# One core, q·kᵀ for 96 heads: the last head's store split between the GpSimd queue and the SP queue

## The chip, the cores and the metric

The kernel runs on one core of one Trainium2 chip. The metric is device time in microseconds (us), lower is better. One profiled execution of the kernel gives the trace; the plain executions give the time.

## The reference

The kernel computes, for every batch and head, the raw attention scores: `out[b,h,i,j] = sum over d of q[b,h,i,d] * k[b,h,j,d]`, in float32, with 8 batches, 12 heads, a sequence of 1024 and a head dimension of 64.

```python
def reference(q, k):
    return np.einsum('bhid,bhjd->bhij', q, k).astype(np.float32)
```

The inputs are 2 x 25 MB, the output is 96 heads x 1024 x 1024 x 4 bytes, some 403 MB. There is no softmax and no scaling: nearly all bytes that the kernel moves are the output's.

## The kernel before

**Heads and blocks.** Batch and head are one axis of 96 heads (`of` is the output as 96 x 1024 x 1024). They are handled in blocks of 2, 2, 4, 8, 8 and then six times 12 heads. For each block q and k are loaded (`load`, L66, or `load_head`, L78, for the first two blocks), cast to 16-bit by GpSimd (`cast_rows`, L90; `cast_quads`, L113), transposed (by TensorE for the first two blocks, by VectorE for all others, L145) and then used head by head. The loads of a later block are issued in the midst of an earlier one (`LOADS`, L263), by ScalarE's queue.

**One head.** `scores` (L156) makes the 1024 x 1024 scores of one head in an SBUF tile `o_sb` of 128 partitions x 8 rows x 1024 columns. Partition p holds rows 8p to 8p+7 of the head (the index t in the code), so each partition's 32 KB are contiguous in DRAM. From the second head on the head goes in four steps u = 0 to 3 of two rows t each: eight matmuls fill a PSUM tile of 128 x 2048 (L171), and one ScalarE copy takes it to `o_sb` (L181). After the fourth copy one DMA of 4 MB, issued by SP, stores the head (L184 to L189):

```python
out=of[self.first + n].rearrange("(p t) j -> p (t j)", p=P),
in_=o_sb.rearrange("p t j -> p (t j)"),
```

This is 128 rows of 32 KB, one for each partition, and the trace has them as 128 packets of 32 KB on the 16 DMA engines, eight to an engine.

**What orders the work.** Every instruction is pinned to program order (`pin`), so each engine runs its list as written; the framework only adds the waits. `out_pool` has three buffers, so the first copy of a head waits until the store of the head three before it has landed. SP issues nothing but the stores after the first loads, each behind the wait for its head's last copy. GpSimd's list ends with the casts of the last block. When all lists are at their end, SP waits at the end of the program (L304) for the landing of every DMA, and a barrier of the five engines closes it.

Of the kernel before, what the change touches and what calls it, by code (L numbers as in the profile page):

```python
# [10 lines left out]
P = 128  # L11

@with_exitstack
def kernel(
# [6 lines left out]
    nc = tc.nc  # L21
# [3 lines left out]
    BH = B * H  # L25
# [5 lines left out]
    of = out.rearrange("b h i j -> (b h) i j")  # L31
# [3 lines left out]
    PE_BLOCKS = 2  # L35
    NMAX = max(sizes)
    CHUNK = 48 * 32

    consts = ctx.enter_context(tc.tile_pool(name="consts", bufs=1))
    ident = consts.tile([P, P], F16)  # L40
# [6 lines left out]
    pin = tc.keep_in_program_order  # L47

    def half_tile():
        half_sb = half_pool.tile([P, CHUNK], F16, tag="half")  # L50
        return half_sb

    class Block:
# [3 lines left out]
        def __init__(self, first, N, by_pe):  # L57
# [5 lines left out]
            self.halves = {}  # L63
            self.cut = max(1, self.R * 32 // CHUNK + (self.R * 32 % CHUNK > 0))

# [90 lines left out]
        def scores(self, n, side, ps_pool, w):  # L156

            half, g = divmod(n, self.N // 2)
            cs = slice(half * D, (half + 1) * D)

            qT = self.qT.rearrange("c (g m t) -> c g t m", t=NT, m=P)
            kT = self.kT.rearrange("c (g j) -> c g j", j=S)
            o_sb = out_pool.tile([P, NT, S], F32, tag="out")
            for u in range(NT // w):
                ps = ps_pool.tile([P, w * S], F32, tag="po")
                for tt in range(w):
                    for j in range(2):
                        js = slice(j * 512, (j + 1) * 512)
                        at = tt * S + j * 512
                        pin(  # L170
                            nc.tensor.matmul(  # L171
                                ps[:, at : at + 512],
                                qT[cs, g, w * u + tt],
                                kT[cs, g, js],
                            )
                        )
                dst = o_sb[:, w * u : w * u + w].rearrange("p t j -> p (t j)")
                if w == 1 and u % 2:
                    pin(nc.vector.tensor_copy(out=dst, in_=ps))  # L179
                else:  # L180
                    pin(nc.scalar.copy(out=dst, in_=ps))  # L181
                for do in side.get(u, []):
                    do()
            pin(  # L184
                nc.sync.dma_start(
                    out=of[self.first + n].rearrange("(p t) j -> p (t j)", p=P),
                    in_=o_sb.rearrange("p t j -> p (t j)"),
                )
            )  # L189

    blocks, first = [], 0
    for i, N in enumerate(sizes):
# [116 lines left out]
```

## Time and profile before

| what | value |
|---|---|
| time, median of 3 runs | 1063.17 us (1063.16 to 1063.77) |
| span of the profiled execution, first to last instruction | 1061.2 us |
| median less span | 1.9 us |
| bytes moved, mean rate over the span | 453 MB, 427 GB/s |
| stores | 96 of 4 MB, all by SP; median 21.8 us from issue to landing |
| ScalarE copies to `o_sb` | 384, 1.86 us each for 128 x 2048 |
| TensorE, ScalarE, VectorE, GpSimd busy | 66%, 66%, 44%, 35% |

The profiled execution's own time is its span of 1061.2 us and what lies around it; the plain runs' median is 1.9 us above the span.

The page's slices each cover a fortieth of the span, 26.5 us. The views that the prediction uses are the chain of waits that ends last, the table of stretches (for any stretch of time: what each engine was busy, the share of the 16 DMA engines' time that packets took, and GB/s; a packet is booked where it starts), and the records of single packets and landings on which that table rests. A store's landing is made of 16 records, one for each DMA engine that has finished its part.

### The profile page before, as it was taken

The page shows a single profiled execution, that of the slowest core. Times are in us where ns is not written, and L with a number is a line of the kernel's source. Part 1 is how long each engine was busy: PE and PEld are TensorE (multiplying, and loading weights), DVE is VectorE, ACT ScalarE, POOL GpSimd, SP SyncE. Part 2 cuts the span into 40 slices and gives each one's busy share as a digit, 9 for nine tenths or more (in the row PEclk, how much of TensorE's full clock was granted, in tenths as well). Part 3 has the DMA queues.
Part 4 walks back from the last instruction along what each step waited for, and adds up shares of the span by engine and source line. Part 5 has one row for each costly group of instructions (what it writes and reads, how often), then busy time and mean ns, then how long its engine had stood idle before and what let it go on. Part 6 is the DMA issues. An engine that isn't in the chain of part 4 may idle for free.

```text
span 1061.2 us, 4282 instructions
## 1 busy us (share of the span) xinstructions
PE 701.0 (66%) x1568; PEld 241.5 (23%) x1568; DVE 471.3 (44%) x75; ACT 697.3 (66%) x386; POOL 368.3 (35%) x286
## 2 busy tenths in 40 slices
PE   6866755765677557775577855777557777778770
PEld 2322211221222112221122211222112222222220
DVE  2999502990795007960079600795007950000000
ACT  4866755755677556775577755777557777777771
POOL 6967228607720463304633046320463200000000
DMA  9999999999999999999999999999999999999997
GB/s 375 434 435 434 434 432 429 432 430 429 429 434 431 429 438 429 435 422 428 434 434 433 425 424 437 432 431 426 432 430 434 434 434 430 430 435 430 433 431 319
DMA packets 17588, 453.25 MB, mean 427 GB/s; under 512 B 1952, under 2 KB 1952, under 8 KB 2976
## 3 DMA queue, kind: packets, MB, share of 16 engines
q1 hardware_dynamic: 14688, 406.85, 89.2%
q10 hardware_dynamic: 2880, 46.14, 10.3%
q8 instruction: 12, 0.20, 0.1%
q14 instruction: 8, 0.07, 0.0%
HBM read 50.33 MB, written 402.65 MB: 427 GB/s over the span
## 4 chain that ended last, share of the span: by engine, by line
DMA 71%; ACT 18%; PE 8%; issue 1%; DVE 0%; POOL 0%; ACTq 0%; SPq 0%
DMA out_dram<-o_sb 71%; ACT o_sb L181 18%; PE ps L171 8%; DMA early<-in_q_dram 0%; PE ps L151 0%; POOL half_sb L97 0%; ACTq L181 0%; DVE kT L154 0%; DVE o_sb L179 0%; ACT kT L154 0%; SPq L84 0%
## 5 line engine op out<-in xcount | busy, mean ns | idle before, releaser
L181 ACT COPY o_sb<-ps 128x2048 f32<-128x2048 f32 (+1 forms) x384 | 695.0, 1860 | 334.6 <-DMA out_dram<-o_sb 306.2
L171 PE MATMUL ps<-kT,qT 64*128 64x512 f16 x1536 | 696.9, 617 | 329.2 <-ACT o_sb L181 325.5
L127 POOL CAST half_sb<-x_sb 32x1536 f16<-32x1536 f32 (+1 forms) x256 | 346.5, 1353 | 454.5 <-DMA x_sb<-in_q_dram 315.0
L171 PEld LDWEIGHTS <-qT 64*128 64x128 f16 x1536 | 238.3, 157 | 786.0 <-issue 781.3
L145 DVE STREAM_TRANSPOSE qT<-half_sb 128x1536 f16<-128x1536 f16 (+1 forms) x34 | 232.7, 7140 | 372.0 <-issue 314.9
L145 DVE STREAM_TRANSPOSE kT<-half_sb 128x1536 f16<-128x1536 f16 (+1 forms) x34 | 234.3, 7198 | 0.0
L127 POOL CAST half_sb<-early 32x1024 f16<-32x1024 f32 x16 | 16.5, 1034 | 3.9 <-DMA early<-in_q_dram 3.2
L151 PE MATMUL ps<-ident,half_sb 128*128 128x128 f16 x32 | 4.1, 308 | 6.6 <-POOL half_sb L97 6.0
L154 DVE COPY qT<-ps 128x1024 f16<-128x1024 f16 x2 | 2.5, 1225 | 12.1 <-PE ps L151 12.1
L179 DVE COPY o_sb<-ps 128x1024 f32<-128x1024 f32 x4 | 4.9, 1224 | 4.3 <-PE ps L171 4.3
L97 POOL CAST half_sb<-early 128x512 f16<-128x512 f32 x8 | 4.6, 613 | 4.1 <-DMA early<-in_q_dram 4.1
L151 PEld LDWEIGHTS <-half_sb 128*128 128x128 f16 x32 | 3.2, 139 | 8.4 <-POOL half_sb L97 6.3
L154 ACT ACT_TABLE_LOAD x1 | 1.3, 1283 | 5.6 <-DMA early<-in_q_dram 5.6
L154 DVE COPY kT<-ps 128x1024 f16<-128x1024 f16 x1 | 1.2, 1225 | 4.3 <-PE ps L151 4.3
L154 ACT COPY kT<-ps 128x1024 f16<-128x1024 f16 x1 | 1.0, 1012 | 1.2 <-PE ps L151 1.2
masks.py:199 POOL TENSOR_SCALAR_AFFINE_SELECT ident<-ident 128x128 f16<-128x128 f16 x1 | 0.3, 292 | 0.1
masks.py:197 POOL MEMSET ident<- 128x128 f16 x1 | 0.2, 204 | 0.3 <-POOLq L293 0.3
L293 POOL MEMSET const-float32-0.0<- 128x1 f32 x1 | 0.1, 98 | 0.2 <-issue 0.2
L293 POOL MEMSET const-bfloat16-1.0<- 128x1 bf16 x1 | 0.1, 100 | 0.0
L293 POOL MEMSET const-uint8-127<- 128x1 uint8 x1 | 0.1, 100 | 0.0
L293 POOL MEMSET const-float32-1.0<- 128x1 f32 x1 | 0.1, 98 | 0.0
## 6 DMA issues: line engine op xcount, KB each, us to landing
out_dram<-o_sb SPq DMA_DIRECT2D x96, 4096.0 KB, 21.8
x_sb<-in_q_dram ACTq DMA_DIRECT2D x6, 3072.0 KB, 22.2
x_sb<-in_k_dram ACTq DMA_DIRECT2D x6, 3072.0 KB, 21.9
x_sb<-in_k_dram ACTq DMA_DIRECT2D x2, 2048.0 KB, 19.0
x_sb<-in_q_dram SPq DMA_DIRECT2D x1, 2048.0 KB, 18.2
x_sb<-in_q_dram ACTq DMA_DIRECT2D x1, 2048.0 KB, 18.5
early<-in_k_dram ACTq DMA_DIRECT2D x4, 256.0 KB, 5.0
early<-in_q_dram SPq DMA_DIRECT2D x4, 256.0 KB, 4.7
```

The source lines that it names most:

```text
L97: nc.gpsimd.tensor_copy(out=self.rows[x][:, :, half], in_=self.raw[x][:, half * n : (half + 1) * n].rearrange("p (r d) -> p r d", d=D),)
L127: nc.gpsimd.tensor_copy(out=half_sb[q0 : q0 + 32].rearrange("p (r d) -> p r d", d=32), in_=raw[32 * b : 32 * b + 32, c * m : (c + 1) * m, h],)
L145: pin(nc.vector.transpose(out=dst, in_=src))
L151: pin(nc.tensor.transpose(t_ps[:, t], self.rows[x][:, t], ident))
L154: pin(copy(out=dst, in_=src))
L171: nc.tensor.matmul(ps[:, at : at + 512], qT[cs, g, w * u + tt], kT[cs, g, js],)
L179: pin(nc.vector.tensor_copy(out=dst, in_=ps))
L181: pin(nc.scalar.copy(out=dst, in_=ps))
L293: nc = _bacc.Bacc("TRN2", target_bir_lowering=False, num_devices=1)
```

## The change

For all heads but the last nothing changes: the store is moved into a method of its own, `store`, with the same DMA. For the last head the eight rows t of a partition are seen as `(g h t)` with g, h and t of two each: h = 0 are the rows 0, 1, 4, 5 (made by the copies u = 0 and u = 2), h = 1 are the rows 2, 3, 6, 7 (u = 1 and u = 3).

- The rows h = 0 are stored by two DMAs that GpSimd issues: first for the partitions 126 and 127 (4 pieces of 8 KB), then for the partitions 0 to 125 (252 pieces of 8 KB).
- The rows h = 1 of all 128 partitions are stored by one DMA that SP issues (256 pieces of 8 KB).

The two GpSimd DMAs wait for the third copy of the last head, SP's DMA for the fourth, as the store before did. GpSimd's list gets two instructions longer, SP's keeps its length; no other engine's list changes. At the end SP also waits for the landing of the two GpSimd DMAs.

```diff
+    TAIL = ((126, 128), (0, 126))
...
-            pin(
-                nc.sync.dma_start(
-                    out=of[self.first + n].rearrange("(p t) j -> p (t j)", p=P),
-                    in_=o_sb.rearrange("p t j -> p (t j)"),
-                )
-            )
+            self.store(n, o_sb)
+
+        def store(self, n, o_sb):
+            if self.first + n < BH - 1:
+                pin(
+                    nc.sync.dma_start(
+                        out=of[self.first + n].rearrange("(p t) j -> p (t j)", p=P),
+                        in_=o_sb.rearrange("p t j -> p (t j)"),
+                    )
+                )
+                return
+            dst = of[self.first + n].rearrange(
+                "(p g h t) j -> p g h (t j)", g=2, h=2, t=2
+            )
+            src = o_sb.rearrange("p (g h t) j -> p g h (t j)", g=2, h=2)
+            for a, b in TAIL:
+                pin(nc.gpsimd.dma_start(out=dst[a:b, :, 0], in_=src[a:b, :, 0]))
+            pin(nc.sync.dma_start(out=dst[:, :, 1], in_=src[:, :, 1]))
```

## The prediction

> **What bounds the kernel now.** I read the page from the top, then the chain that ended last, then the last 40 us in stretches.
>
> ```profile
> GB/s 375 434 435 434 434 432 429 432 430 429 429 434 431 429 438 429 435 422 428 434 434 433 425 424 437 432 431 426 432 430 434 434 434 430 430 435 430 433 431 319
> q1 hardware_dynamic: 14688, 406.85, 89.2%
> DMA 71%; ACT 18%; PE 8%; issue 1%; DVE 0%; POOL 0%; ACTq 0%; SPq 0%
> L181 ACT COPY o_sb<-ps 128x2048 f32<-128x2048 f32 (+1 forms) x384 | 695.0, 1860 | 334.6 <-DMA out_dram<-o_sb 306.2
> ```
>
> The stores bound it. The DMA engines move 422 to 438 GB/s in every slice between the first and the last, ScalarE's copies wait for a free output buffer, and the chain is 71% store. Only two slices fall short: the first and the last, 319 GB/s. At 430 GB/s the last slice's bytes would have taken 319/430 x 26.5 = 19.7 us, so 6.8 us are lost there, and the change touches only this slice.
>
> SP's waits, and the timeline of the last matmuls and copies, say the same:
>
> ```profile
> SPq L304 <- DMA out_dram<-o_sb: 21.0, 1, 21.0
> ```
>
> ```profile
> 1034.96 1.86 PE L171 MATMUL ps<-kT,qT 64*128 64x512 f16 x4
> 1035.09 3.64 ACT L181 COPY o_sb<-ps 128x2048 f32<-128x2048 f32 x2 [0.18 <-PE ps L171]
> 1038.75 0.33 SPq L185 DMA_DIRECT2D out_dram<-o_sb  x1
> ```
>
> All computing is done at 1038.73. The last store is issued at 1038.75, and SP then waits 21.0 us for landings. A 4 MB store takes 9.7 us at 430 GB/s, so more than one store's worth was still queued in front of it. So the last store does not wait for its issue; it waits for its turn. The stretches (columns: stretch, its length, busy time of PE, PEld, DVE, ACT, POOL, clock, DMA share, GB/s) show how the queue empties:
>
> ```profile
> 1051.00:1052.00 1.00, 0.00 (x0) 0.00 (x0) 0.00 (x0) 0.00 (x0) 0.00 (x0) 1.00 0.91 393
> 1052.00:1053.00 1.00, 0.00 (x0) 0.00 (x0) 0.00 (x0) 0.00 (x0) 0.00 (x0) 1.00 0.91 393
> 1053.00:1054.00 1.00, 0.00 (x0) 0.00 (x0) 0.00 (x0) 0.00 (x0) 0.00 (x0) 1.00 0.61 262
> 1054.00:1055.00 1.00, 0.00 (x0) 0.00 (x0) 0.00 (x0) 0.00 (x0) 0.00 (x0) 1.00 0.38 164
> 1055.00:1056.00 1.00, 0.00 (x0) 0.00 (x0) 0.00 (x0) 0.00 (x0) 0.00 (x0) 1.00 0.15 66
> 1056.00:1057.00 1.00, 0.00 (x0) 0.00 (x0) 0.00 (x0) 0.00 (x0) 0.00 (x0) 1.00 0.08 33
> 1057.00:1058.00 1.00, 0.00 (x0) 0.00 (x0) 0.00 (x0) 0.00 (x0) 0.00 (x0) 1.00 0.08 33
> 1058.00:1059.00 1.00, 0.00 (x0) 0.00 (x0) 0.00 (x0) 0.00 (x0) 0.00 (x0) 1.00 0.08 33
> 1059.00:1060.00 1.00, 0.00 (x0) 0.00 (x0) 0.00 (x0) 0.00 (x0) 0.00 (x0) 1.00 0.00 0
> ```
>
> 33 GB/s over 1 us is one 32 KB packet. So from 1056 on one packet starts in each microsecond, and by the packet records (1213 ns for 32 KB) all three belong to one DMA engine: it starts its last packets at 1056.16, 1057.37 and 1058.58 and is done at 1059.80. The engine before it is done at 1057.02, the next two at 1056.67 and 1055.87, eight have finished by 1053.8, and the mean of all 16 is 1054.7. The late engine is not a hiccup of the last store: in the landing records it comes 6.7 to 6.9 us after the first engine in each of the last eight stores. It has the same bytes, and enters the last store late. This engine alone sets the end.
>
> After its last packet come the landing at 1060.26 and the closing barrier, to 1061.24: 1.44 us that the change leaves in place. The plain median, 1063.17, is 1.93 us above this span; I make the sum on the span and add 1.93.
>
> **The change, part by part.**
>
> *What the split removes.* SP's last DMA halves: eight packets of 32 KB on each engine become 16 of 8 KB. The early loads show 8 KB packets at 309 ns. Four of them are 1236 ns against 1213 (consecutive packets overlap by some 3.5 ns in either size, so 1222 against 1209.5), that is 12.5 ns more for each 32 KB. A whole store in such pieces costs each engine 8 x 12.5 ns = 0.1 us more. The SP issue itself, 0.33 us at 1038.75, is hidden: the late engine is busy with earlier stores until about 1050.1, the others until 1043.4 or later.
>
> *What the earlier issue brings.* GpSimd's DMAs wait for the third copy (done at 1036.86) instead of the fourth (1038.73): 1.9 us earlier. Worth nothing: DMA share is 0.9 or more up to 1053, so no engine lacks work at that time. GpSimd's list is empty from before 900 us on; nothing stands behind its two DMAs but the closing barrier. Issuing costs GpSimd an unknown time. The nearest rows are SP's issue (0.33 us) and the 256 KB loads on an idle chip, 4.7 to 5.0 us from issue to landing. I take 3 us from the row's 4.7, all hidden: until an engine runs dry without the GpSimd half there are 1053.1 - 4.9 - 1036.9 = 11.3 us, and until it moves the end some 17 us. Were that cover gone, each us beyond it would be a us of time.
>
> *What the two DMAs cost an engine.* Here is the gain or the loss. Total bytes and the engines' speed stay; what can move the end is how the GpSimd half is dealt to the 16 engines. Evenly it is eight partitions each, 16 pieces, 16 x 305.5 ns = 4.89 us. 126 partitions do not go evenly into 16, and no row of this trace shows a GpSimd DMA, so I bound the late engine's share. At best it gets none of the 126: it is 4.89 us earlier, done at 1054.9, and the end passes to the next engine. At worst GpSimd uses few engines: 126 = 14 x 9 = 9 x 14 = 7 x 18, and with 18 partitions an engine carries 36 pieces, 11.0 us instead of 4.89.
>
> The value I take: 14 engines with nine partitions each and the other two partitions on two engines apart, since this is the most even equal split of 126 and nearest to the observed eight to an engine. Then 14 engines have one partition more (2 x 0.31 = 0.62 us later) and two have seven fewer (14 x 305.5 ns = 4.28 us earlier). If the late engine is one of the two, it ends at 1059.80 - 4.28 + 0.1 = 1055.6, and the engine now second sets the end: 1057.02 + 0.62 + 0.1 = 1057.74. That is 2.06 us earlier. At the end SP has one more semaphore to look at, 0.08 us by the gaps between its last waits. Sum: -2.06 + 0.08 = -1.98; the span becomes 1059.26, the time 1061.2 us.
>
> [...]
>
> [...]
>
> **The rivals.**
>
> *A. The late engine keeps its share or nearly so.* For: two of 16 engines are relieved, 14 are not, and nothing in the trace tells which the late one is. Against: the split is uneven, so some engine gains. With nine partitions on it: +0.62 + 0.1 + 0.08 = +0.8, 1064.0 us; with six, -4 x 305.5 ns + 0.18 = -1.0, 1062.1 us.
>
> *B. Slower: GpSimd deals the 126 over few engines.* With nine engines of 14 partitions each carries 12 pieces more, 3.7 us; with seven, 20 pieces more, 6.1 us. If the late engine is among them the end moves by 3.8 to 6.3 us (1067.0 to 1069.5); if not, the one at 1057.02 may be: +1.0 to +3.5 us. It decides from the point at which the late engine carries eight pieces (four partitions) more than now, 12 or more in all. For: 126 is an odd size. Against: the equal split over 14 exists.
>
> *C. GpSimd's half comes late, or the program pays for it elsewhere.* If its first packet reaches the engines after some 1054, the end goes with it; a GpSimd path with a cost of 2 to 5 us outside the covered stretch (at the start, or in the closing barrier) would give 1063 to 1066. Against: the 11 us of cover. For: no row prices it.
>
> *D. Nothing of it shows,* because the halves are dealt as the store was: +0.1 + 0.08, 1063.4 us.
>
> **How the numbers follow.** 0.2% of 1063.17, 2.1 us, is about what a measurement of this kernel can tell from no change; below 1061.0 is faster, above 1065.3 slower. Forecast (late engine relieved by far): 0.44, 1060.2 to 1061.8, the low end if the second engine is relieved too (end at 1056.67 + 0.72, -0.35 more) and the pieces cost nothing, plus some change of the lags between executions. Its centre lies just short of 2.1 us, so I count 0.33 as faster (perfect levelling would end at 1054.7, 5.1 us earlier, which bounds any gain) and 0.11 as within. A and D: 0.32, within. B: 0.14, slower. C: 0.10, of it 0.07 slower. Together: faster 0.33, within 0.11 + 0.32 + 0.03 = 0.46, slower 0.14 + 0.07 = 0.21. The range 1060.2 to 1066.0 leaves out perhaps 0.03 below and 0.16 above. The forecast's own range is 1060.2 to 1061.8.
>
> **What would show it.** Right: in the stretches after, the run of single packets at the end is shorter and starts earlier, the last packet ends near 1057.7, SP's last wait is some 19 us, and on GpSimd's queue two engines have two packets of 8 KB each and 14 have 18. Wrong: a tail of 8 KB packets, four to a 1.2 us, past 1059.8 (A), a GpSimd queue that uses few engines (B), GpSimd packets that begin only after 1048 (C), or a longer closing barrier (C). It would also be wrong if the engine that is late in the profiled execution were not the late one in the plain ones.

## The result and the profile after

The changed kernel is slower: 1065.78 us in the median of 18 runs (1064.39 to 1069.24), against 1063.22 us before (1063.01 to 1063.77). The ratio is 1.0025, with a 95% interval of 1.0018 to 1.0031. That is +2.6 us where -2.0 us was forecast. The runs also scatter over 4.9 us, where those of before scatter over 0.8. The profiled execution of after is one of its faster ones (1064.82 us, span 1062.8), so its +1.6 us of span is less than the median's loss.

What answers to the page's lines of before:

```profile
GB/s 375 434 433 433 433 433 434 434 424 433 437 431 426 430 430 432 434 427 427 434 434 432 421 431 433 432 433 425 429 432 432 433 434 432 431 434 430 431 433 292
q1 hardware_dynamic: 14816, 404.76, 88.6%
q0 software_dynamic: 352, 2.10, 0.5%
DMA 71%; ACT 18%; PE 8%; issue 1%; DVE 0%; POOL 0%; ACTq 0%; SPq 0%
```

Between the first slice and the last the rate is 421 to 437 GB/s, as before (422 to 438), and the last slice falls from 319 to 292 GB/s. q0 is GpSimd's queue: 2.10 MB, the half h = 0, in 352 packets, of which 256 are data (8 KB) and 96 carry 4 bytes.

The issues stand in the timeline, and SP's last wait in its waits:

```profile
1034.98 3.63 ACT L182 COPY o_sb<-ps 128x2048 f32<-128x2048 f32 x2 [0.18 <-PE ps L172]
1037.16 1.45 POOL L201 DMA_DIRECT2D out_dram<-o_sb  x2 [205.76 <-ACT o_sb L182]
1038.64 0.64 SPq L202 DMA_DIRECT2D out_dram<-o_sb  x1
```

```profile
SPq L317 <- DMA out_dram<-o_sb: 21.9, 1, 21.9
```

GpSimd issues its two DMAs in 1.45 us, SP its half in 0.64 us; neither is late. SP waits 21.9 us at the end instead of 21.0. The stretches show what happens in that wait (length, busy times of the engines, clock, DMA share, GB/s). Before:

```profile
1045.00:1053.00 8.00, 0.00 (x0) 0.00 (x0) 0.00 (x0) 0.00 (x0) 0.00 (x0) 1.00 0.98 422
1053.00:1057.00 4.00, 0.00 (x0) 0.00 (x0) 0.00 (x0) 0.00 (x0) 0.00 (x0) 1.00 0.31 131
1057.00:1061.00 4.00, 0.00 (x0) 0.00 (x0) 0.00 (x0) 0.00 (x0) 0.00 (x0) 1.00 0.04 16
```

After:

```profile
1045.00:1053.00 8.00, 0.00 (x0) 0.00 (x0) 0.00 (x0) 0.00 (x0) 0.00 (x0) 1.00 0.93 350
1053.00:1057.00 4.00, 0.00 (x0) 0.00 (x0) 0.00 (x0) 0.00 (x0) 0.00 (x0) 1.00 0.83 301
1057.00:1061.00 4.00, 0.00 (x0) 0.00 (x0) 0.00 (x0) 0.00 (x0) 0.00 (x0) 1.00 0.16 68
```

Look at the two last columns together. From 1045 to 1053 the packets of after take 93% of the engines' time, nearly as before, but move 350 GB/s instead of 422. The engines are occupied and move less. By 1053 they are (422 - 350) x 8 = 576 KB behind, 1.4 us of all 16 engines at 420 GB/s.

The packet records say how. Before, from 1036 on, none of the 242 packets of 32 KB takes longer than 1.24 us. After, 112 of 625 data packets are stretched: more than 13% over the 309 ns of 8 KB or the 1213 ns of 32 KB, up to 1.11 us for 8 KB and 2.38 us for 32 KB. Stretched are packets of both queues, SP's 32 KB packets of the store before too.

The last data packet ends at 1060.93 instead of 1059.80: +1.13 us. From there to the end of the span it is 1.91 us instead of 1.45: +0.46, most of it one gap of 0.37 us between SP's last wait and its step into the closing barrier. Together they are the span's +1.6.

### The profile page after: what moved, and what is told of

The parts are those of the page before. It is cut to its first block, busy times and chain, and to the rows that moved or that the text cites. A ratio compares the mean times of both kernels' runs of the same rounds, so it can differ in the third digit from the quotient of the medians.

```text
span 1062.8 us, 4285 instructions
## 1 busy us (share of the span) xinstructions
PE 700.8 (66%) x1568; PEld 241.6 (23%) x1568; DVE 471.7 (44%) x75; ACT 697.1 (66%) x386; POOL 369.8 (35%) x288
## 4 chain that ended last, share of the span: by engine, by line
DMA 71%; ACT 18%; PE 8%; issue 1%; DVE 0%; POOL 0%; ACTq 0%; SPq 0%
DMA out_dram<-o_sb 71%; ACT o_sb L182 18%; PE ps L172 8%; DMA early<-in_q_dram 0%; PE ps L152 0%; POOL half_sb L98 0%; ACTq L182 0%; DVE kT L155 0%; DVE o_sb L180 0%; ACT kT L155 0%; SPq L85 0%
```

## The experiments

All times are medians; the ratio is to the kernel before on the same chip in the same hour (1062.94 to 1063.13 us). GB/s are those of the stretch 1045 to 1053, stretched packets those from 1036 on, as above (912 ns for 24 KB, 611 ns for 16 KB). Both columns belong to the one profiled execution, which is not always near the median: 1064.82 us for the change, but 1068.57 for e4 (median 1066.17) and 1069.29 for f2 (1067.16). So they show whether packets are stretched, and rank the versions only roughly.

| run | last head's store | time, us | ratio (95%) | GB/s | stretched |
|---|---|---|---|---|---|
| before | SP: 128 partitions | 1063.22 | 1 | 422 | 0 of 242 |
| after | GpSimd: 2 + 126, half; SP: 128, half | 1065.78 | 1.0025 (1.0018 to 1.0031) | 350 | 112 of 625 |
| e1_hw_two | SP: 128 twice, halves | 1063.59 | 1.0005 (0.9996 to 1.0013) | 417 | 0 of 631 |
| e2_act_half | ScalarE: 128, half; SP: 128, half | 1063.15 | 1.0001 (0.9992 to 1.0010) | 415 | 0 of 631 |
| e3_pool_even | GpSimd: 128, half; SP: 128, half | 1063.46 | 1.0005 (0.9996 to 1.0014) | 410 | 0 of 632 |
| e4_pool_rev | GpSimd: 126 + 2, half; SP: 128, half | 1066.17 | 1.0034 (1.0021 to 1.0046) | 330 | 143 of 636 |
| f1_sp_uneven | SP: 2 + 126, half; SP: 128, half | 1069.78 | 1.0061 (1.0048 to 1.0074) | 293 | 130 of 633 |
| f2_pool_112_16 | GpSimd: 112 + 16, half; SP: 128, half | 1067.16 | 1.0038 (1.0024 to 1.0052) | 313 | 158 of 625 |
| f3_sp_120_8 | SP: 120 + 8, whole rows | 1070.92 | 1.0074 (1.0062 to 1.0087) | 229 | 93 of 247 |
| f4_pool_mid | the change at head 47 | 1078.04 | 1.0140 (1.0126 to 1.0153) | - | - |
| g1_sp_120_only | SP: 120, whole rows, 8 left out | 1068.92 | 1.0054 (1.0040 to 1.0068) | 250 | 89 of 246 |
| g2_sp_64_64 | SP: 64 + 64, whole rows | 1069.86 | 1.0069 (1.0054 to 1.0085) | 242 | 97 of 249 |
| g3_pool_quarter | GpSimd: 2 + 126, quarter; SP: 128, rest | 1064.73 | 1.0016 (1.0007 to 1.0025) | 337 | 98 of 372 |
| g4_pool_all | GpSimd: 2 + 126, whole rows | 1069.47 | 1.0059 (1.0046 to 1.0071) | 238 | 95 of 244 |
| h1_sp_dram_halves | SP: 128 twice, other places in DRAM | 1063.65 | 1.0006 (0.9996 to 1.0015) | 414 | 0 of 365 |

### Issuer, pieces, queues, or the dealing

Four suspects: the GpSimd queue itself, two queues on one engine, the 8 KB pieces, and the dealing of 2 and 126 partitions. Three runs each keep some of them and deal all 128 partitions at once.

e1_hw_two:

```diff
-            for a, b in TAIL:
-                pin(nc.gpsimd.dma_start(out=dst[a:b, :, 0], in_=src[a:b, :, 0]))
+            pin(nc.sync.dma_start(out=dst[:, :, 0], in_=src[:, :, 0]))
```

> The last head's two halves both go out by SP, each in one DMA of 128 partitions and 256 pieces of 8 KB; nothing by GpSimd. Theory 1 (GpSimd's queue is what costs: its packets beside SP's on the same engines, and its dealing): 1063.2 to 1063.5, as before plus 0.1 to 0.2 for the smaller pieces. Theory 2 (two queues on one engine cost, whoever issues): the same, 1063.2 to 1063.5. Theory 3 (pieces of 8 KB in place of 32 KB cost): 1065 to 1066, as slow as the changed kernel.

Measured: 1063.59 us, no stretched packet; 8 KB packets take 320 ns at most. The pieces are not the cause.

e2_act_half:

```diff
-            for a, b in TAIL:
-                pin(nc.gpsimd.dma_start(out=dst[a:b, :, 0], in_=src[a:b, :, 0]))
+            pin(nc.scalar.dma_start(out=dst[:, :, 0], in_=src[:, :, 0]))
```

> The half h = 0 goes out by ScalarE's queue in one DMA of 128 partitions, the half h = 1 by SP as in the changed kernel; nothing by GpSimd. Theory 1 (GpSimd's queue costs): 1063.2 to 1063.6. Theory 2 (two queues on one engine cost, whoever issues): 1065 to 1066, and GB/s at the end falls to some 340 as in the changed kernel. Theory 3 (small pieces): 1065 to 1066.

Measured: 1063.15 us (+0.1 us, interval -0.9 to +1.1), no stretched packet. Two queues with small pieces on the same engines cost nothing that can be seen; theory 2 falls.

e3_pool_even:

```diff
-            for a, b in TAIL:
+            for a, b in ((0, 128),):
```

> GpSimd stores the half h = 0 in one DMA of all 128 partitions, so that each of the 16 engines gets eight; SP's half as in the changed kernel. Theory 1a (GpSimd's queue costs in itself): 1065 to 1067, GB/s of some 340 at the end. Theory 1b (it is the uneven dealing of 126 and 2 partitions that costs): 1063.2 to 1063.8.

Measured: 1063.46 us. GpSimd's queue is there, with the same 2.10 MB, but with 16 packets of 4 bytes instead of 96:

```profile
q0 software_dynamic: 272, 2.10, 0.5%
1045.00:1053.00 8.00, 0.00 (x0) 0.00 (x0) 0.00 (x0) 0.00 (x0) 0.00 (x0) 1.00 0.97 410
```

410 GB/s, no stretched packet, +0.5 us (interval -0.4 to +1.5): neither GpSimd as the issuer nor a fixed cost of its DMAs explains the loss. What is left of the change is the split into 126 and 2 partitions.

e4_pool_rev:

```diff
-    TAIL = ((126, 128), (0, 126))
+    TAIL = ((0, 126), (126, 128))
```

> The changed kernel with GpSimd's two DMAs in the other order, partitions 0 to 125 first. If the dealing goes round the engines from where the last DMA ended, other engines carry less: the time moves by 1 us or more, either way, against the changed kernel (1065.8). If the deal is fixed (eight partitions to an engine, six to the last) or does not matter, 1065 to 1066.5 as the changed kernel.

Measured: 1066.17 us, 0.4 us from the changed kernel and within its scatter, with 143 stretched packets. An effect of the order is not seen: the intervals of the two ratios overlap. The records of this run show the dealing, though: where an engine's packets can be followed from end to start, four engines have exactly 18 GpSimd pieces, nine partitions. With 126 partitions that fits 14 engines with nine each, and two without; the other engines could not be followed cleanly.

### What it is about the dealing

f1 and f2 separate the two things that go together in 126 + 2: GpSimd's handling of an odd number, and partitions that are dealt to the engines in another way than in a DMA of 128, here called out of step. No record names the partition that a packet reads: how partitions are dealt follows from numbers of pieces and from the version, not from a view.

f1_sp_uneven:

```diff
-                pin(nc.gpsimd.dma_start(out=dst[a:b, :, 0], in_=src[a:b, :, 0]))
+                pin(nc.sync.dma_start(out=dst[a:b, :, 0], in_=src[a:b, :, 0]))
```

> The changed kernel with its two uneven DMAs (partitions 126-127, then 0 to 125) issued by SP instead of GpSimd. Theory 1b-i (an engine that gets nine partitions instead of its usual eight reads out of step with the others and stalls, whoever issues): packets of 8 KB stretched over 350 ns as in the changed kernel, GB/s near 340 at the end, 1064.5 to 1067. Theory 1b-ii (it takes GpSimd's way of dealing an odd size, with its many 4-byte packets): no stretched packets; then the time shows only the dealing: 1063.7 to 1064.2 if the late engine is among the 14 with nine partitions, 1060.5 to 1061.5 if it is one of the two left out.

Measured: 1069.78 us, above the 1067 that theory 1b-i allowed, with 130 stretched packets. Beside e1, with the same issuer and the same pieces, only the split into 2 and 126 differs, and it costs 6 us. So the loss does not need GpSimd. Why it is 4 us larger through SP is open.

f2_pool_112_16:

```diff
-    TAIL = ((126, 128), (0, 126))
+    TAIL = ((0, 112), (112, 128))
```

> GpSimd stores the half in two DMAs of 112 and 16 partitions: seven and one for each engine, an even eight in all, but not the eight partitions that each engine has in a DMA of 128. Theory 1b-i (out of step with the usual partitions): stretched packets, 1064.5 to 1067. Theory 1b-ii (GpSimd's odd dealing over 14 and 2 engines): no stretched packets, no additional 4-byte packets, 1063.0 to 1063.8. A cost of having two GpSimd DMAs at all would also show here: above 1064.

Measured: 1067.16 us, just above the 1067 of theory 1b-i. Seven and one partitions for each engine are an even eight in all (the engines that can be followed to their end have 16 GpSimd pieces), GpSimd's queue has only 32 packets of 4 bytes, and still 158 packets are stretched:

```profile
q0 software_dynamic: 288, 2.10, 0.6%
1045.00:1053.00 8.00, 0.00 (x0) 0.00 (x0) 0.00 (x0) 0.00 (x0) 0.00 (x0) 1.00 0.99 313
```

So neither the unequal shares nor the many 4-byte packets are needed for the loss. What is left is that the half goes out in DMAs of fewer than 128 partitions, out of step with the others.

f3_sp_120_8 was meant to relieve the late engine, with eight partitions on each of 15 engines, and no GpSimd:

```diff
-            for a, b in TAIL:
-                pin(nc.gpsimd.dma_start(out=dst[a:b, :, 0], in_=src[a:b, :, 0]))
-            pin(nc.sync.dma_start(out=dst[:, :, 1], in_=src[:, :, 1]))
+            dst = of[self.first + n].rearrange("(p t) j -> p (t j)", p=P)
+            src = o_sb.rearrange("p t j -> p (t j)")
+            for a, b in ((0, 120), (120, 128)):
+                pin(nc.sync.dma_start(out=dst[a:b], in_=src[a:b]))
```

> The last head goes out whole by SP, 32 KB pieces, in DMAs of the partitions 0 to 119 and of the other eight. If 120 goes over 15 engines with eight each and the late engine is the one left out: it ends 9.7 us earlier and the next at 1057.0 or, with one of the last eight pieces, 1058.2; 1060.3 to 1061.7. If the late engine is among the eight that get one piece more: 1064.1 to 1064.4. If it is among the other seven: 1063.0 to 1063.3.

Measured: 1070.92 us, outside of all that was expected. Packets of 32 KB take up to 4.9 us:

```profile
1045.00:1053.00 8.00, 0.00 (x0) 0.00 (x0) 0.00 (x0) 0.00 (x0) 0.00 (x0) 1.00 0.93 229
1053.00:1057.00 4.00, 0.00 (x0) 0.00 (x0) 0.00 (x0) 0.00 (x0) 0.00 (x0) 1.00 0.84 254
1057.00:1061.00 4.00, 0.00 (x0) 0.00 (x0) 0.00 (x0) 0.00 (x0) 0.00 (x0) 1.00 0.79 188
```

A share of 0.93 at 229 GB/s: at the rate before, 422 GB/s at a share of 0.98, these bytes would have taken a share of 0.53. More than 40% of the occupied time is stretch.

f4_pool_mid:

```diff
-            if self.first + n < BH - 1:
+            if self.first + n != BH // 2 - 1:
```

> The three DMAs of the change, but for head 47 in the middle of the run; the last head's store is as before. What a program pays for having GpSimd DMAs at all (at the start or in the closing barrier) stays in, the cost at the end goes. Theory 1b (uneven dealing at the end): 1063.0 to 1064.0, the loss in the middle is mostly taken up by the queue of stores, up to 1 us of it stays with the late engine. If a fixed cost of GpSimd's DMAs were the cause: 1065 to 1066.

Measured: 1078.04 us, outside both. It does not answer its question: in the middle of the run GpSimd has casts of a later block in front of its DMAs, and they wait for VectorE. GpSimd issues the half store only at 567.6 us, it lands at 585.2, and ScalarE waits for the buffer:

```profile
ACT o_sb L182 <- DMA out_dram<-o_sb: 25.6, 1, 25.6
```

The question is answered by e3_pool_even: a fixed cost of GpSimd's DMAs is within its +0.5 us (at most 1.5 by the interval).

### 120 alone, 64 + 64, and the dose

In f3 the last eight partitions also went out, over eight engines by the count of packets (SP's queue has 14695, seven more than before: 15 and eight landings instead of 16). g1_sp_120_only leaves these out of the output (256 KB less are stored):

```diff
-            for a, b in ((0, 120), (120, 128)):
-                pin(nc.sync.dma_start(out=dst[a:b], in_=src[a:b]))
+            pin(nc.sync.dma_start(out=dst[:120], in_=src[:120]))
```

> The last head's partitions 0 to 119 go out by SP in one DMA, whole 32 KB rows; the rows of the partitions 120 to 127 are left out of the output, so 256 KB are not stored at all. Theory P (each engine needs its own group of partitions as in a DMA of 128; any other number of partitions deals them differently, two engines meet at one group and wait): packets stretched over 1.4 us, GB/s well below 400 at the end, 1064 to 1070 although less is stored. Theory C (only the eight-partition DMA, eight engines on one group of partitions, stalled the version with 120 and 8): no stretched packets, 1060.3 to 1063.2.

Measured: 1068.92 us, 6 us slower with less work; theory C falls. SP's queue has 14679 packets against 14688 before, eight of data and one of 4 bytes fewer, so this store has 15 engines' landings instead of 16. Dealt evenly, that is eight partitions on each of 15 engines, where a DMA of 128 has them on 16.

g2_sp_64_64, an even split by partitions:

```diff
-            for a, b in ((0, 120), (120, 128)):
+            for a, b in ((0, 64), (64, 128)):
```

> The last head goes out by SP in two DMAs of the partitions 0 to 63 and 64 to 127, whole 32 KB rows: four partitions for each engine twice, a perfectly even deal by bytes. Theory P (the groups of partitions that the engines meet at): 16 engines read from half of the partitions, so about half of the rate, packets stretched to 2 us and more, up to 9.7 us more for 4 MB: 1067 to 1073. Rival U (it is unequal numbers of partitions for the engines that cost): 1063.0 to 1063.6.

Measured: 1069.86 us; rival U falls.

```profile
1045.00:1053.00 8.00, 0.00 (x0) 0.00 (x0) 0.00 (x0) 0.00 (x0) 0.00 (x0) 1.00 1.01 242
1053.00:1057.00 4.00, 0.00 (x0) 0.00 (x0) 0.00 (x0) 0.00 (x0) 0.00 (x0) 1.00 0.94 279
1057.00:1061.00 4.00, 0.00 (x0) 0.00 (x0) 0.00 (x0) 0.00 (x0) 0.00 (x0) 1.00 0.96 221
```

All 16 engines take part in both DMAs (SP's queue has 16 packets of 4 bytes more than before), they are occupied nearly all the time, and the rate is 242 GB/s, 57% of the 422 before, and stays below 280 to the end. Part of the store before is still in this stretch. The versions whose DMAs all cover 128 partitions move 410 to 417 GB/s in the same stretch (e1, e2, e3). So the rate goes with the set of partitions that a DMA covers; how the engines reach the partitions, and whether two of them wait for each other at one group, as theory P has it, no run shows.

g3_pool_quarter and g4_pool_all change the dose, the part of the head that goes through GpSimd's 2 + 126: a quarter, and all of it. In g3 that part also starts earlier (first data packet at 1038.66 us instead of 1042.35), since the rows 0 and 1 are ready after the first copy.

g3_pool_quarter:

```diff
-                pin(nc.gpsimd.dma_start(out=dst[a:b, :, 0], in_=src[a:b, :, 0]))
-            pin(nc.sync.dma_start(out=dst[:, :, 1], in_=src[:, :, 1]))
+                pin(nc.gpsimd.dma_start(out=dst[a:b, : 2 * S], in_=src[a:b, : 2 * S]))
+            pin(nc.sync.dma_start(out=dst[:, 2 * S :], in_=src[:, 2 * S :]))
```

> The change with half the dose: GpSimd's two DMAs store only the rows 0 and 1 of each partition (8 KB, a quarter of the head), SP the rows 2 to 7 in one DMA of 128 partitions and 24 KB pieces. Theory P: the part that is out of step is halved; about half of the cost of the change: 1063.8 to 1064.8, fewer stretched packets. If a cost of two odd GpSimd DMAs at all: 1065 to 1066.5, as the change.

g4_pool_all:

```diff
-                pin(nc.gpsimd.dma_start(out=dst[a:b, :, 0], in_=src[a:b, :, 0]))
-            pin(nc.sync.dma_start(out=dst[:, :, 1], in_=src[:, :, 1]))
+                pin(nc.gpsimd.dma_start(out=dst[a:b], in_=src[a:b]))
```

> The change with twice the dose: GpSimd stores the whole last head, the partitions 126-127 and then 0 to 125, in 32 KB pieces; SP stores nothing of it. Theory P: twice the part out of step, 1067 to 1071, GB/s at the end below 340. If the cost were that two queues of small pieces meet on one engine: 1063 to 1064.5, since SP's queue has only the earlier stores.

Measured: 1064.73 and 1069.47 us. By the ratios a quarter costs 1.7 us, a half (the change) 2.7, the whole 6.3. The cost grows with the bytes that are dealt out of step, very roughly as they do. In g4 there are no small pieces and SP's queue has only earlier stores, and it is the dearest of the three. The dose is not all that differs, though: in both runs the engines that can be followed carry eight of GpSimd's packets, one for a partition, so eight partitions and not nine, and GpSimd's queue has 48 packets of 4 bytes, not 96. These engines have as many partitions as in a DMA of 128, and their packets are stretched all the same (in g4 six of the eight on one engine take 2.4 us or more instead of 1.21).

### SBUF or DRAM

A row of SBUF partition p goes to one place in DRAM, so all these versions also wrote DRAM in another order. h1_sp_dram_halves reads all 128 partitions in each DMA, as the store before, and writes DRAM like g2, first the lower 2 MB of the head, then the upper; the rows of the last head land in another order:

```diff
-            for a, b in ((0, 64), (64, 128)):
-                pin(nc.sync.dma_start(out=dst[a:b], in_=src[a:b]))
+            dst = of[self.first + n].rearrange("(a p r) j -> a p (r j)", a=2, p=P)
+            src = o_sb.rearrange("p (a r) j -> a p (r j)", a=2)
+            for i in range(2):
+                pin(nc.sync.dma_start(out=dst[i], in_=src[i]))
```

> The last head goes out by SP in two DMAs of all 128 partitions, four rows of each (16 KB pieces); the first DMA writes the first 2 MB of the head in DRAM and the second the other 2 MB, as the two DMAs of 64 partitions did, so the rows of this head land in another order in the output. SBUF is read as in the store before, DRAM is written as in the version with 64 and 64. If engines meet at groups of SBUF partitions: no stretched packets, 1063.0 to 1063.6. If the order in which DRAM is written was what stalled: stretched packets, 1067 to 1071.

Measured: 1063.65 us, no stretched packet:

```profile
1045.00:1053.00 8.00, 0.00 (x0) 0.00 (x0) 0.00 (x0) 0.00 (x0) 0.00 (x0) 1.00 0.97 414
```

So it is not the halves of DRAM: writing them one after the other costs nothing that can be seen (+0.6 us, interval -0.4 to +1.6) when all 128 partitions are read at once. That leaves the SBUF side. Which engine writes which place within a half was not held apart, so this last step is by exclusion.

## Why the prediction was wrong, point by point

- **What bounds the kernel, and what the tail is.** Right, but for a rounding: the 16 engines' mean end is 1054.8, not 1054.7. Up to the last slice hardly anything moved, and the end is still set by one late engine: in the profile after, its last packets are three of 8 KB, from 1060.01 to 1060.93, when all others are done by 1059.8.
- **The pieces, 0.1 us.** Right in kind: e1 has no 8 KB packet over 320 ns. The 0.1 us itself is too small to be told from its +0.5 us (interval -0.4 to +1.4).
- **The earlier issue and GpSimd's issuing.** Right that they are hidden. The first GpSimd data packet starts at 1042.35, 5.2 us after the issue, not 3, and within the 11.3 us of cover.
- **14 engines with nine partitions.** Nine is right on the engines that can be followed (18 pieces on each of four in e4, and on the late one here); that 14 have nine and two were left out fits the 126 and is the estimate that the forecast's -2.06 us rests on, but no run shows it. The late engine was not left out: after its earlier stores it alternates between 8 KB packets of GpSimd's and SP's queue until 1059.70. It carries 18 of GpSimd's pieces. So rival A's condition held, and its sign, a tail of 8 KB packets past 1059.8, is there: one more partition and the pieces, +0.72 us, are the larger part of the +1.13 that its end moved; one stretched packet of its own, 784 ns instead of 309, makes up the rest. The prediction had named and priced this. But A's price was 1064.0 us, and the median is 1.8 us above it. A's other case, six partitions on the late engine, no run shows: the engines that can be followed have nine, in g3 and g4 eight. Which engines the plain runs left out is not recorded.
- **"Total bytes and the engines' speed stay."** This is the step that failed. The bytes stayed; the speed did not. It fell from 422 to 350 GB/s in the stretch in which both queues were busy. I took the 309 and 1213 ns of a packet as properties of its size. They held in every version whose DMAs all cover 128 partitions (e1, e2, e3, h1); dealt in another way, packets took up to 1.1 us (8 KB) and 2.4 us (32 KB). This undoes the forecast even without A: it had the second engine done at 1057.74, and in the profile two engines besides the late one end only at 1059.70 and 1059.75. So with the late engine left out altogether the last data packet would, by these records, still have ended at about 1059.75, against 1059.80 before.
- **The range.** That 1065.78 lies within 1060.2 to 1066.0 is luck: its upper part was there for rival C and the mild end of rival B, and neither happened.
- **Rival B** expected slower for another reason, few engines with many pieces. As far as it can be followed, the dealing was the even one that B counted against itself (18 pieces on an engine, not 28 or 36), and it was slower all the same.
- **Rival C.** The closing barrier was longer by 0.46 us in the profile. The same gap is in e1 (1.88 us from the last data packet to the end), which has no GpSimd DMA, and not in e3 (1.52 us), which has one. So it does not come with GpSimd; what it comes with is open. GpSimd's first packets came before 1048, so C's other form did not happen either.
- **Relieving the late engine at all.** The arithmetic behind the forecast, an end at 1057.7 once the late engine is relieved, was not brought about by any of the versions tried: each that gave some engine fewer partitions (126, 120) also stretched the packets of others, and ended slower than before by 1.7 us or more. No version was found that beats the kernel before.

## What to carry to other kernels

Where the DMA engines are busy all the time, as here at 421 to 438 GB/s, try first to keep every store from SBUF at all 128 partitions and to split it along the row, if it has to be split: here that cost nothing that could be seen with any of three issuers (+0.1 to +0.6 us), while splits by partitions (2 + 126, 112 + 16, 120 + 8, 64 + 64) of half or all of a 4 MB store cost 2.6 to 7.9 us. An even deal by bytes was no protection (112 + 16: 4.0 us, 64 + 64: 7.3 us). In a profile, read DMA share and GB/s together: a high share at a low rate, here 0.93 at 350 GB/s, went with packets that took longer than their size takes elsewhere (8 KB up to 1.11 us instead of 0.309), and a packet time taken from undisturbed rows was then too short.

## What the runs showed of the hardware that was not expected

- A store of 120 partitions that leaves out 6% of the bytes is 0.54% of the whole kernel slower than one of 128: the 32 KB packets around it took up to 4.6 us, where none takes over 1.24 before.
- In two DMAs of 64 partitions 97 of 249 packets of 32 KB were stretched, up to 3.6 us, and the rate was 242 GB/s instead of 422.
- GpSimd's queue has 16 packets of 4 bytes for one DMA of 128 partitions, 32 for the pair of 112 and 16, 96 for the pair of 126 and 2 in the change, and 48 for the same pair in g3 and g4.
- On the engines that can be followed, GpSimd dealt 126 partitions in two ways: nine to an engine in the change (18 pieces of 8 KB on the late engine), where each partition's half is two separate pieces, and eight to an engine in g3 and g4 (eight packets), where it is one.
